# Recurrent layer: the score products of a chunk as two products of 64 stationary columns each

## The chip, the cores and the metric

The kernel runs on one core of a Trainium2 chip. The metric is the device time of one execution in microseconds; shown are the median of three runs and one execution under the hardware profiler, which gives the trace. TensorE is called PE in the profile (its weight loads PEld), VectorE DVE, ScalarE ACT, GpSimd POOL, SyncE SP.

## The reference, cut to what matters

A streaming encoder of two layers, 512 positions of width 1024. Layer 0 mixes by RWKV-7 (12 heads of 64) beside an attention into 256 memory tokens, layer 1 by chunked attention; each is followed by a conv-GLU. The change lies in the recurrent mixer of layer 0:

```python
def step(state, inp):
    r_t, w_t, k_t, v_t, a_t, b_t = inp
    sa = jnp.einsum('bhvk,bhk->bhv', state, a_t)
    state = (state * w_t[:, :, None, :] + sa[..., None] * b_t[:, :, None, :]
             + v_t[..., None] * k_t[:, :, None, :])
    return state, jnp.einsum('bhvk,bhk->bhv', state, r_t)
...
_, ys = lax.scan(step, s0, xs)
```

## The kernel before, in words

The kernel doesn't step through positions. It cuts the 512 positions into 8 chunks of 64 and makes, for each chunk and head, the four 64 by 64 score blocks between the keys (b and k, divided by the decay) and the queries (a and r, times the decay); the state then goes from chunk to chunk. Two heads make a pair, head 0 in partitions 0 to 63 and head 1 in partitions 64 to 127, and there are six pairs.

Each pair goes through three generators. `prepare` (line 574) projects r, k, v, and fills the tiles `AR` (queries: slot 0 is a, slot 1 is r) and `KB` (keys: slot 0 is k, slot 1 is b, slot 2 a copy of k, made by ScalarE on line 659); it also inverts the small triangular blocks on VectorE, lines 665 to 677, with transfers to DRAM and back around them. `front` (line 715) makes the score products on line 725, masks them with the constant `m1` into the tile `ML` on VectorE (line 728), and transposes keys, queries and values on lines 739, 749 and 751. `back` (line 776) makes the products with `ML` (among them lines 789, 797, 813, 824), runs over the chunks and hands the pair on.

On line 725 the stationary operand of one product is 64 partitions by 128 columns: two neighbouring slots of `KB`, slots 1 and 2 (b, k) for head 0 and slots 0 and 1 (k, b) for head 1. The moving operand is `AR` with both slots, 128 columns. The output is one of two PSUM banks, one for each head, 128 partitions by 128 columns for each of four chunks. So b lands in the head's own partitions and k in those of the other head. `front` runs the loop twice, for chunks 0 to 3 and 4 to 7 (`c4`); this makes 16 products a pair and 96 in all. All operands are fp32. Lines 749 and 751 are of another shape: 64 stationary and 64 moving columns, the first with the output in the head's own partitions, the second with it in the other head's.

`weave` (line 82) interleaves the generators by costs that are written beside each `yield`: in each of five stages it runs `back` of pair i-1, `front` of pair i and `prepare` of pair i+1. The framework then places the instructions on each engine by its own priorities and dependences; on each engine they run in the order so fixed. The pool `ps_s`, of which the score products take two banks, has four banks while this layer runs. The layer's remainder on TensorE is dense products (`dense`, lines 198, 199, 203), which take the projections of the next pair.

Of the kernel before, what the change touches and what calls it, by code (L numbers as in the profile page):

```python
# [111 lines left out]
def trunk_kernel(ctx, tc, A, out):  # L112
    nc = tc.nc
    PE, V, SC, GP = nc.tensor, nc.vector, nc.scalar, nc.gpsimd
# [19 lines left out]
    def C(name, lo=0, n=None):  # L134
        o, w = COFF[name]
        return cst[:, o + lo:o + lo + (w if n is None else n)]
# [7 lines left out]
    def ps_s(shape=(P, S)):  # L144
        return banks["S"].tile(list(shape), F32, name="pss", tag="pss")
# [7 lines left out]
    def ups():  # L153
        return ps_s((P, 8, 64))
# [224 lines left out]
    HS = (top, bot)  # L379
# [26 lines left out]
    def kt_(name, shape=(P, S), bufs=None, dt=F32):  # L406
        if bufs is None:
            return kp.tile(list(shape), dt, name=name, tag=name)
        return kp.tile(list(shape), dt, name=name, tag=name, bufs=bufs)
# [139 lines left out]
    def c3(ap):  # L549
        return ap.rearrange("p (c t) -> p c t", c=NCH)  # L550
# [164 lines left out]
    def front(i, T):  # L715
        v, KB, AR, Tt = c3(T["v"]), T["KB"], T["AR"], T["Tt"]

        ML = kt_("ML", (P, 2, NCH, 192), bufs=2)

        for c4 in range(2):  # L720
            ps = [ps_s((P, 4, 128)) for _ in range(2)]
            for c in range(4):
                cc = c4 * 4 + c
                for h in range(2):
                    PE.matmul(ps[h][:, c], KB[HS[h], cc, 1 - h:3 - h].rearrange("p s t -> p (s t)"),
                              AR[HS[h], cc].rearrange("p s t -> p (s t)"), start=True, stop=True)
            for h in range(2):
                V.tensor_tensor(ML[:, h, c4 * 4:c4 * 4 + 4, 0:128], ps[h][:],  # L728
                                C("m1").unsqueeze(1).to_broadcast([P, 4, 128]), op=ALU.mult)
            yield 1000  # L730
        Rq = kt_("Rq", (P, 8, 64), bufs=2)
        SC.copy(Rq[:], AR[:, :, 1, :])
        VT = kt_("VT", (P, 3, NCH, 64), bufs=2)

        def rows_kb():
            ps = [ups(), ups()]
            for c in range(8):
                for h in range(2):
                    PE.transpose(ps[h][:, c], KB[HS[h], c, 1 - h:3 - h].rearrange("p s t -> p (s t)"),
                                 cst[HS[h], I64:I64 + 64])  # L740
            for h in range(2):
                SC.copy(ML[:, h, :, 128:192], ps[h][:])


        def rows_av():
            ps = [ups(), ups()]
            for c in range(8):
                for h in range(2):
                    PE.matmul(ps[h][HS[h], c], AR[HS[h], c, 0], cst[HS[h], I64:I64 + 64], start=True, stop=True)
                for h in range(2):  # L750
                    PE.matmul(ps[h][HS[1 - h], c], v[HS[h], c], C("blkc", h * 64, 64)[HS[h]], start=True, stop=True)
            for h in range(2):
                SC.copy(VT[:, h], ps[h][:])

        rows_av()
        yield 1000
        rows_kb()
        yield 800
        T.update(Rq=Rq, ML=ML, VT=VT)
# [157 lines left out]
    for st_ in range(NPAIR - 1):  # L917
        gens = [(front(st_, Ts[st_]), 1.069 * FRONT_COST), (prepare(st_ + 1, Ts[st_ + 1]), .971 * PREP_COST)]
        if st_ > 0:
            gens.insert(0, (back(st_ - 1, Ts[st_ - 1], dst_mix), 1.003 * BACK_COST))  # L920
        weave(gens, tc)
# [39 lines left out]
    def later(ns):  # L961
        yield 0, ns

    a_, b_ = NPAIR - 2, NPAIR - 1
    weave([(told(back(a_, Ts[a_], dst_mix), "back"), 1.5 * BACK_COST),
           (chain(front(b_, Ts[b_]), later(25000), back(b_, Ts[b_], dst_mix, other_tiles, lambda: "back" in over)),
            1.5 * (FRONT_COST + BACK_COST)),
           (told(chain(q_mem(lambda f: A["wA"][18 + f], hact, qmA), flush_mix(), mA), "mem"),
# [336 lines left out]
```

## Time and profile before

| | us |
|---|---|
| median of three runs (lowest, highest) | 1363.49 (1362.89, 1365.41) |
| the profiled execution | 1366.57 |
| its span in the trace | 1364.8 |
| TensorE busy in the span | 1316.1 |
| VectorE busy in the span | 825.4 |
| ScalarE busy in the span | 615.1 |

A row of a timeline merges neighbouring instructions of one line: its length goes from the first start to the last end, and x16 says that it holds 16 records. An fp32 product leaves two records, each with a weight load of its own. Matmul starts are measured, their ends are modelled, so that the distance between starts tells more than the length of one record. "128*64 64x128" in a row is the stationary operand's partitions and columns, then the moving operand's. The stage of the recurrent layer lies between some 84 and 350 us.

### The profile page before, as it was taken

What the parts mean: (1) busy time and instruction counts of PE and PEld (TensorE: products, weight loads), DVE (VectorE), ACT (ScalarE), POOL (GpSimd) and SP (SyncE); (2) the same over time, 40 slices, a digit from 0 to 9 for tenths busy, and PEclk for the clock granted to TensorE, in tenths of its full rate; (3) what the DMA queues carried; (4) which work ended last, traced back from release to release, by engine and by line L of the source; (5) the groups of instructions that cost most, each with busy time, mean ns of one, the idle gap of its engine ahead of it and who ended that gap; (6) DMA issues with size and microseconds to landing.
All of it is one profiled execution on the core that took longest, in us unless ns stands there. A gap on an engine that the chain in (4) does not pass through costs nothing.

```text
span 1364.8 us, 20881 instructions
## 1 busy us (share of the span) xinstructions
PE 1316.1 (96%) x8266; PEld 1070.6 (78%) x8266; DVE 825.4 (60%) x1751; ACT 615.1 (45%) x1025; POOL 35.5 (3%) x57
## 2 busy tenths in 40 slices
PE   6989999999999999999999999999999999999996
PEld 5777777776788888888888878786888888888886
DVE  7876888778475556555334675757666555653324
ACT  6556565555444333333222476657443333332221
POOL 3000000000000000000000000000000000000000
PEclk9999999999999999999999999999999999999998
DMA  5366544555222322232233422232322232233332
GB/s 183 113 188 130 108 99 106 116 109 132 81 91 93 102 100 93 94 106 88 85 87 112 131 86 93 86 116 63 108 93 93 95 106 93 93 94 88 106 85 75
DMA packets 64322, 140.49 MB, mean 103 GB/s; under 512 B 24672, under 2 KB 28896, under 8 KB 64224
## 3 DMA queue, kind: packets, MB, share of 16 engines
q1 hardware_dynamic: 61200, 128.15, 30.0%
q0 software_dynamic: 3024, 11.01, 4.6%
q8 instruction: 65, 1.06, 0.3%
q14 instruction: 33, 0.27, 0.1%
HBM read 132.32 MB, written 6.82 MB: 102 GB/s over the span
## 4 chain that ended last, share of the span: by engine, by line
PE 78%; DVE 12%; ACT 4%; DMA 3%; issue 2%; SPq 1%; DVEq 0%; ACTq 0%; POOLq 0%
PE psf L198 12%; PE psf L199 12%; PE psf L203 12%; PE psd L198 10%; PE psd L199 10%; PE psd L203 10%; DVE Xu L675 2%; DVE Xs L677 1%; PE pss L1122 1%; PE psl L203 1%; DVE Xs L670 1%; DVE ML L728 1%; PE pss L297 1%; PE psd L1072 1%; PE pss L1108 1%
## 5 line engine op out<-in xcount | busy, mean ns | idle before, releaser
L175 DVE TENSOR_TENSOR wlo<-wraw,whi 128x1024 fp32r<-128x1024 f32 (+1 forms) x181 | 216.5, 1196 | 132.5 <-PE psd L203 118.2
L169 ACT CAST whi<-wraw 128x1024 fp32r<-128x1024 f32 (+1 forms) x202 | 207.8, 1030 | 162.2 <-DMA wraw<-in_ffn_out_dram 40.1
L198 PE MATMUL psf<-r2h,whi 128*128 128x512 f32 x352 | 137.1, 390 | 0.0
L198 PE MATMUL psf<-r1h,whi 128*128 128x512 f32 x352 | 137.1, 390 | 0.0
L199 PE MATMUL psf<-r1l,whi 128*128 128x512 f32 x352 | 137.0, 389 | 0.0
L199 PE MATMUL psf<-r2l,whi 128*128 128x512 f32 x352 | 136.9, 389 | 0.0
L198 PE MATMUL psd<-r1h,whi 128*128 128x512 f32 x318 | 127.4, 401 | 1.2 <-ACT whi L169 1.2
L199 PE MATMUL psd<-r1l,whi 128*128 128x512 f32 x318 | 124.9, 393 | 0.0
L203 PE MATMUL psd<-r1h,wlo 128*128 128x512 f32 x318 | 86.7, 405 | 4.4 <-DMA wlo<-in_wA_dram 4.4
L199 PE MATMUL psd<-f3l,whi 128*128 128x512 f32 (+1 forms) x238 | 88.6, 377 | 0.0
L198 PE MATMUL psd<-f3h,whi 128*128 128x512 f32 (+1 forms) x238 | 88.5, 376 | 0.0
L362 DVE TENSOR_TENSOR tmp<-psf,rho 128x512 f32<-128x512 f32 x44 | 30.4, 692 | 94.7 <-PE psf L203 94.7
L203 PE MATMUL psf<-r1h,wlo 128*128 128x512 f32 x352 | 86.9, 389 | 0.0
L203 PE MATMUL psf<-r2h,wlo 128*128 128x512 f32 x352 | 86.9, 389 | 0.0
L198 PE MATMUL psd<-r2h,whi 128*128 128x512 f32 (+1 forms) x200 | 77.1, 389 | 0.8 <-ACT r2h L1129 0.7
L199 PE MATMUL psd<-r2l,whi 128*128 128x512 f32 (+1 forms) x200 | 76.3, 384 | 0.8 <-DVE r2l L216 0.8
L203 PEld LDWEIGHTS psf<-r2h,wlo 128*128 128x128 f32 x352 | 66.1, 188 | 13.7
L199 PEld LDWEIGHTS psf<-r1l,whi 128*128 128x128 f32 x352 | 66.1, 188 | 13.7
L203 PEld LDWEIGHTS psf<-r1h,wlo 128*128 128x128 f32 x352 | 66.1, 188 | 13.7
L199 PEld LDWEIGHTS psf<-r2l,whi 128*128 128x128 f32 x352 | 66.1, 188 | 13.7
L198 PEld LDWEIGHTS psf<-r2h,whi 128*128 128x128 f32 x352 | 66.1, 188 | 13.6
L198 PEld LDWEIGHTS psf<-r1h,whi 128*128 128x128 f32 x352 | 66.1, 188 | 13.6
(369 smaller groups left out, 2442.3 us busy)
## 6 DMA issues: line engine op xcount, KB each, us to landing
wraw<-in_ffn_in_dram SPq DMA_DIRECT2D x88, 512.0 KB, 3.2
wraw<-in_ffn_out_dram SPq DMA_DIRECT2D x32, 448.0 KB, 3.3
wraw<-in_wA_dram SPq DMA_DIRECT2D x20, 512.0 KB, 3.9
wlo<-in_wA_dram POOLq DMA_DIRECT2D x17, 512.0 KB, 7.9
wraw<-in_w_out_dram SPq DMA_DIRECT2D x16, 512.0 KB, 3.4
wraw<-in_ffn_out_dram SPq DMA_DIRECT2D x16, 512.0 KB, 4.5
wraw<-in_wB_dram SPq DMA_DIRECT2D x8, 512.0 KB, 3.3
Lr<-d SPq DMA_DIRECT2D x24, 128.0 KB, 5.4
```

What stands on the lines that cost most here:

```text
L169: SC.copy(hi[:, :n], raw)
L175: V.tensor_tensor(lo[:, :n], raw, hi[:, :n], op=ALU.subtract)
L198: PE.matmul(ps, wh[:, j * P:(j + 1) * P], ah, start=start and n == 0, stop=False)
L199: PE.matmul(ps, wh[:, j * P:(j + 1) * P], al, start=False, stop=False)
L203: PE.matmul(ps, wl[:, j * P:(j + 1) * P], act(k)[0], start=False, stop=stop and n == len(ks) - 1)
L297: PE.matmul(pso[hs, :], vm[l][:, kt, (f * 2 + hh) * 64:(f * 2 + hh + 1) * 64], pts[f, hh, kt], start=kt == 0, stop=kt == 1)
L362: V.tensor_tensor(v[:], pv[:], rho[:], op=ALU.mult)
L670: V.scalar_tensor_tensor(X[:, m, q + 1:], L1[:, :, 0], X[:, m, q:q + 1], X[:, m, q + 1:], op0=ALU.mult, op1=ALU.add)
L675: V.tensor_tensor(uv, L1.rearrange("p i o -> p o i").to_broadcast([P, k, n]), X[:, 0:k, q:q + 1].to_broadcast([P, k, n]), op=ALU.mult)
L677: V.tensor_tensor(X[:, 0:k, q + 1:], X[:, 0:k, q + 1:], uv, op=ALU.add)
L728: V.tensor_tensor(ML[:, h, c4 * 4:c4 * 4 + 4, 0:128], ps[h][:], C("m1").unsqueeze(1).to_broadcast([P, 4, 128]), op=ALU.mult)
L1072: PE.matmul(pt, r1h[:, k, ts], wh[:, ws], start=k == 0, stop=False)
```

## The change

In `front`, each product of 128 stationary columns is made as two of 64. For `d` = 0, slot 1 (b) of both heads, with the output in the head's own partitions; for `d` = 1, slot 0 (k) of both heads, with the output in the other head's. The values, the banks and the place of each value stay; the number of products goes from 96 to 192. Slot 2 of `KB` is still read by line 739.

```diff
             for c in range(4):
                 cc = c4 * 4 + c
-                for h in range(2):
-                    PE.matmul(ps[h][:, c], KB[HS[h], cc, 1 - h:3 - h].rearrange("p s t -> p (s t)"),
-                              AR[HS[h], cc].rearrange("p s t -> p (s t)"), start=True, stop=True)
+                for d in range(2):
+                    for h in range(2):
+                        PE.matmul(ps[h][HS[h ^ d], c], KB[HS[h], cc, 1 - d],
+                                  AR[HS[h], cc].rearrange("p s t -> p (s t)"), start=True, stop=True)
             for h in range(2):
                 V.tensor_tensor(ML[:, h, c4 * 4:c4 * 4 + 4, 0:128], ps[h][:],
                                 C("m1").unsqueeze(1).to_broadcast([P, 4, 128]), op=ALU.mult)
```

## Rows read from the trace of the kernel before

**Rows 1.** The page, part 1: engine, busy us (share of the span), instructions.
```profile
PE 1316.1 (96%) x8266; PEld 1070.6 (78%) x8266; DVE 825.4 (60%) x1751; ACT 615.1 (45%) x1025; POOL 35.5 (3%) x57
```

**Rows 2.** Instructions of lines 725 and 813: ns min/median/max, first and last start.
```profile
L725 PEld LDWEIGHTS pss<-AR,xT x192: 182/188/334, 86.8 to 302.2; 64*128 64x128 f32 x192
L725 PE MATMUL pss<-AR,xT x192: 272/272/579, 86.8 to 302.3; 64*128 64x128 f32 x192
...
L813 PEld LDWEIGHTS pss<-VT,Tt x192: 129/133/133, 131.1 to 344.1; 64*64 64x64 f32 x192
```

**Rows 3.** Table by stretch: us, busy us of each engine, PEclk, DMA share, GB/s.
```profile
84.00:350.00 266.00, 249.04 (x3109) 192.68 (x3107) 206.70 (x714) 153.85 (x295) 17.41 (x20) 0.99 0.52 118
120.00:296.00 176.00, 168.13 (x2119) 129.89 (x2119) 139.52 (x489) 101.48 (x184) 11.22 (x13) 1.00 0.50 109
...
97.20:101.20 4.00, 4.00 (x21) 2.93 (x21) 0.00 (x0) 0.55 (x1) 0.16 (x1) 0.50 1.05 278
```

**Rows 4.** Chain that ended last, 84 to 350 us: its shares by line.
```profile
by line: DVE Xu L675 8.8%; DVE Xs L677 7.3%; PE psd L203 5.3%; DVE Xs L670 4.1%; issue 3.9%; DVE ML L728 3.8%; PE psd L198 3.5%; DMA wlo<-in_wA_dram 3.1%; PE psd L199 2.8%; DMA d<-Xs 2.6%; SPq L680 2.5%; DMA Lr<-d 2.5%; PE psl L844 2.1%; PE
```

**Rows 5.** Instructions of line 728, 84 to 350 us, and what they waited for.
```profile
L728 DVE TENSOR_TENSOR ML<-pss,cst x24: 679/684/695, 88.0 to 304.6; 128x512 f32<-128x512 f32 x24
...
  PE pss L725: 4.6, 2
...
DVE ML L728 <- PE pss L725: 4.6, 2, 4.2
```

**Rows 6.** Timeline of PE, 92 to 103 us: start, us, instruction, count, idle before.
```profile
97.18 2.07 PE L203 MATMUL psd<-r1h,wlo 128*128 128x512 f32 x4 [4.44 <-DMA wlo<-in_wA_dram]
99.18 2.08 PE L725 MATMUL pss<-AR,xT 64*128 64x128 f32 x16
101.19 1.90 PE L203 MATMUL psd<-r1h,wlo 128*128 128x512 f32 x4
```

**Rows 7.** Timeline of PE: one burst of lines 725, 813 and 824 each.
```profile
133.24 1.16 PE L725 MATMUL pss<-AR,xT 64*128 64x128 f32 x16
134.34 1.09 PE L813 MATMUL pss<-VT,Tt 64*64 64x128 f32 x16
...
139.21 1.96 PE L824 MATMUL pss<-ML,W 64*64 64x128 f32 x32
```

**Rows 8.** Timeline of PE: lines 749 and 751, first and last records; line 797.
```profile
108.16 0.27 PE L749 MATMUL pss<-cst,AR 64*64 64x64 f32 x2
108.17 0.27 PE L751 MATMUL pss<-cst,xT 64*64 64x64 f32 x2
108.27 0.22 PE L749 MATMUL pss<-cst,AR 64*64 64x64 f32 x2
108.28 0.23 PE L751 MATMUL pss<-cst,xT 64*64 64x64 f32 x2
108.33 0.23 PE L749 MATMUL pss<-cst,AR 64*64 64x64 f32 x2
108.34 0.23 PE L751 MATMUL pss<-cst,xT 64*64 64x64 f32 x2
...
109.10 0.22 PE L751 MATMUL pss<-cst,xT 64*64 64x64 f32 x2
...
126.67 1.15 PE L797 MATMUL pss<-VT,ML 64*64 64x64 f32 x32
```

**Rows 9.** Line 789: a burst in the timeline of PE, and its ns min/median/max.
```profile
211.89 0.69 PE L789 MATMUL pss<-Tl,ML 32*32 32x32 f32 x32
...
L789 PE MATMUL pss<-Tl,ML x160: 191/191/212, 121.9 to 298.2; 32*32 32x32 f32 x160
```

**Rows 10.** Timeline of PE, 122.4 to 124.9 us: order around one burst.
```profile
122.50 0.49 PE L725 MATMUL pss<-AR,xT 64*128 64x128 f32 x2
122.92 0.49 PE L696 MATMUL pss<-tmp,blk 128*128 128x512 f32 x1
123.34 1.16 PE L725 MATMUL pss<-AR,xT 64*128 64x128 f32 x14
```

## The prediction

> **What bounds the kernel now.** I read the page's share of busy time first: TensorE (PE) is busy 96% of the span, VectorE 60% [rows 1]. The bound is TensorE as a whole, but the change touches only line 725, and the shares of a stage are what count. The per-line view gives its place: 192 records between 86.8 and 302.3 us [rows 2]. In the stretch 84 to 350 us TensorE is busy 249.04 of 266 us, so 17 us are idle there, and 9.1 of these lie before 120 us or after 296 us: in 120 to 296 us it is 168.13 of 176 us [rows 3]. So inside the recurrent stage about 95 of each 100 ns taken off TensorE's queue have a chance to count.
>
> But a busy engine is not the same as a path. The chain of waits over that stretch is headed by VectorE's recurrence (lines 675, 677 and 670), and the product's reader, line 728, stands in it with 3.8% [rows 4]. Line 725 is named as what line 728 waited for only twice, 4.6 us in all [rows 5]. And 4.2 of these 4.6 us are one event, which I can place: TensorE idles 4.44 us for a weight transfer, the granted clock is then 0.50 (the lower level, 1.2 GHz) from 97.20 to 101.20 us, and the line-725 burst at 99.18 us takes 2.08 us in place of 1.16 [rows 3, 6, 7]. That wait belongs to a DMA and to the clock after an idle stretch, not to the shape of the products.
>
> **How a burst of line 725 runs today.** Each fp32 product shows as two records. A burst (four chunks, two heads) is 16 records and lasts 1.16 us from its first start to its last modelled end [rows 7]; there are 12 of them: eight in this form, three with the first product split off, one at the low clock. The last record alone is 0.27 us, so 15 distances between starts fill 0.89 us. The lines beside it give the pace: line 813 has the same 128 moving columns with 64 stationary ones, also 16 records, and takes 1.09 us; line 824, of the same form, takes 1.96 us for 32 [rows 7]. The 16 further records cost 0.87 us, 0.109 us for a pair, one record of each head. That the records of a pair run side by side and not after one another is seen in rows 8, where neighbours start 0.01 us apart and the next group 0.06 us later. So the array is full before the change: its upper 64 rows by 128 columns hold one head, the lower 64 rows the other. The change lets four products of half the width run in the place of two; it doesn't lower the number of columns that are streamed.
>
> **The change part by part.**
>
> *Removed: the wide weight loads.* A load of 128 stationary columns takes 188 ns (median) in line 725, one of 64 takes 133 ns in line 813 [rows 2]. Only the first load of a burst is exposed, since the following ones run beside products. Its gain is 188 - 133 = 55 ns a burst. The comparison of whole bursts says the same: 1.16 - 1.09 = 0.07 us [rows 7], 55 ns of it the first load and the rest, 15 ns over seven further pairs, the pairs' slightly closer spacing.
>
> *Added: 96 products, thus 192 records and 192 loads.* The trace of before has the exact form, at half the moving width: lines 749 and 751 put two heads on the diagonal quadrants and then on the other two, in the order in which the change does it. There the four records start at 108.16 and 108.17 us and the next four at 108.27 and 108.28, then at 108.33 and 108.34, 0.06 us a group; 64 records go from 108.16 to the last start at 109.10 us, plus 0.22 us [rows 8]. Line 797, with the same 64 moving columns on two quadrants only, takes 1.15 us for 32 records [rows 8]. So 64 records on four quadrants take 109.10 + 0.22 - 108.16 = 1.16 us, as long as 32 on two: the second pair is free except for about 0.01 us once at each burst's end. I take 0.02 us a burst for it, the upper end by these rows.
>
> *The sum on TensorE.* A burst goes from 1.16 to 1.09 + 0.02 = 1.11 us, 0.05 us less. Twelve bursts make 0.6 us, and the one at the low clock counts twice: 0.65 us.
>
> *What of this reaches the end.* Lower end 0: where VectorE's recurrence paces the step, the products only end 0.05 us earlier into a queue that is late anyway. Upper end 0.65 us: TensorE paces all. TensorE is busy 168.13 of 176 us, but VectorE leads the chain [rows 3, 4]; I lie nearer to the first and take 0.4 us.
>
> *What doesn't move.* Line 728 reads the same two banks with the same shape (684 ns, 24 of them) [rows 5]; the rows of a bank come in the same places, so ScalarE and VectorE get no new work, and no transfer is added. The third copy in the key tile is still needed by the transposes of line 739; only the products stop reading it. The loads and products of line 739, which follow, are unchanged.
>
> *A rule against it.* The row for the cost of a product that is too small to fill its slot is line 789's: 32 records of 32 columns in 0.69 us, of which 0.19 is the last record, so 0.50 us for 31 distances, 16 ns a record [rows 9]. That is a floor that a crowd of small products pays, and it is far under the 27 ns a record that four quadrants with 128 columns would need (0.109 us by four). The Trainium skill, TensorEngine Tiling (Array Packing), section Performance Considerations, says that every matmul carries an overhead of about 60 cycles and warns against tiling along a dimension that is already small. By that page, as an estimate, 192 more products of 60 cycles at 2.4 GHz would add 4.8 us; here the streamed dimension isn't made smaller, and the 64 records in 1.16 us speak against it.
>
> **Rivals.**
>
> *A, the order of TensorE's queue is drawn anew and comes out worse (slower).* The engines' orders are not those of the code: one product of a burst stands at 122.50 us, then a product of line 696, and the remaining 14 records from 123.34 us [rows 10]. The framework places each instruction by its own idea of when it is due, and 96 more products shift that idea for everything behind them. What such a placement can cost is shown by the event at 92 to 101 us: 4.44 us idle, and then 4.00 us at half clock, which loses 2.0 us [rows 3, 6]; 6.4 us together. One more such event gives 1363.5 + 6.4 = 1369.9; half of one, 1366.7. It decides from 2.7 us of additional idle time on TensorE between 84 and 350 us, where 17 us are now. For it: the slack is small and the stage couples five engines. Against: nine of the twelve bursts of line 725 keep together as they are written, and dense products stand around all of them that any order can use as filling.
>
> *B, the same redraw comes out better.* At most the event at 92 to 101 us goes away: 1363.5 - 6.4 = 1357.1; half, 1360.3. Nothing in the change shortens that transfer, so less likely than A.
>
> *C, the second pair does not run beside the first when 128 columns stream.* Both column halves read the same 64 rows' operand. If they take turns, each burst gets eight more pairs of 0.109 us, 0.87 us less the 0.05: 12 x 0.82 = 9.8 us, thus 1373.3. If they run side by side but each of the 192 added records shows the 16 ns of line 789 [rows 9], it is 3.1 us: 1366.6. (The overhead that the Trainium skill's tiling page states, above, would act in this way.) Rows 8 speak clearly against it; what is left is that the width there is 64.
>
> **How the numbers follow.** The profiled execution takes 1366.57 us, its span 1364.8, and the median of the three runs is 1363.49. The sum is 0.4 us off the profiled one, 1366.2, and likewise off the median: 1363.1. Chances: forecast 0.67 (1362.8 to 1363.5, and some 0.7 us to each side for the spread of a median), A 0.16, B 0.10, C 0.07. Low end 1360.0 and high end 1367.5 leave out the outer parts of A, B and C, about 2 in 10; the likeliest case alone holds 1362.1 to 1364.2. A run can tell about 0.2%, 2.7 us. Faster by more than that: B, 0.10. Slower: A and C, 0.23. The same: 0.67.
>
> **What the next profile would show.** Right: line 725 with 384 records of about 270 ns and loads of about 133, bursts of 32 records in 1.10 to 1.11 us, groups of four starts some 0.11 us apart. Wrong on C: bursts near 1.95 us. Wrong on A or B: the bursts are right, and TensorE's idle time between 84 and 350 us has moved by over 2.7 us from 17. If idle time and bursts stay and the time moves all the same, the bound was read wrongly.

## The result and the profile after

The changed kernel takes 1376.66 us (median of 22 runs, 1370.19 to 1383.08) against 1366.32 us for the kernel before on the same chip: ratio 1.0071, 95% interval 1.0057 to 1.0084. It is some 10 us slower; forecast was 0.4 us less, too little to tell from nothing. The profiled execution takes 1375.35 us, its span is 1373.6.

The page, part 1, and the product's own line (ns min/median/max, first and last start), with one burst from TensorE's timeline:

```profile
PE 1321.7 (96%) x8458; PEld 1074.5 (78%) x8458; DVE 825.6 (60%) x1751; ACT 616.1 (45%) x1025; POOL 35.2 (3%) x57
...
L726 PEld LDWEIGHTS pss<-AR,xT x384: 129/133/228, 86.3 to 305.3; 64*64 64x64 f32 x192
L726 PE MATMUL pss<-AR,xT x384: 268/269/473, 86.3 to 305.4; 64*64 64x128 f32 x192
...
168.12 1.10 PE L726 MATMUL pss<-AR,xT 64*64 64x128 f32 x32
```

The product (line 726 now; everything behind it moved down by one line) behaves as the change says: 384 records for 192, loads of 133 ns for 188 [rows 2], and a burst of 32 records in 1.10 us for 16 in 1.16 [rows 7]. The bursts show nothing of the loss. The stretches show where it is (us, busy us of each engine, PEclk, DMA share, GB/s), after:

```profile
84.00:350.00 266.00, 245.52 (x3129) 188.56 (x3129) 200.53 (x698) 149.08 (x280) 17.41 (x20) 0.95 0.52 118
...
166.00:208.00 42.00, 37.47 (x542) 29.82 (x542) 32.73 (x112) 23.90 (x44) 2.59 (x3) 0.96 0.43 93
208.00:252.00 44.00, 41.64 (x563) 33.02 (x562) 35.04 (x124) 25.09 (x45) 2.59 (x3) 0.96 0.46 100
252.00:296.00 44.00, 40.30 (x554) 31.95 (x554) 34.36 (x121) 24.52 (x44) 2.59 (x3) 0.96 0.48 102
...
324.00:328.20 4.20, 3.06 (x26) 2.07 (x27) 4.15 (x16) 2.04 (x8) 0.86 (x1) 1.00 0.69 166
328.20:341.90 13.70, 13.70 (x58) 7.53 (x56) 6.82 (x25) 6.71 (x22) 0.00 (x0) 0.50 0.36 70
```

Read the PEclk column, third from the end. Before, the clock was 0.99 between 84 and 350 us and 1.00 from 120 to 296 [rows 3]. Now it is 0.96 in each of three stages, and then 0.50 for 13.7 us on end, from 328.2 us. TensorE's idle time from 84 to 350 us is 266 - 245.52 = 20.5 us for 17.0. Three of its waits, from TensorE's timeline (the bracket is the idle time before the row, and who ended it):

```profile
183.49 1.05 PE L558 MATMUL pss<-cst,tmp 128*128 128x2 f32 x8 [1.75 <-ACT tmp L633]
...
272.15 1.05 PE L558 MATMUL pss<-cst,tmp 128*128 128x2 f32 x8 [1.84 <-ACT tmp L633]
...
326.15 0.33 PE L845 MATMUL psl<-W,MQ 64*64 64x64 f32 x4 [1.14 <-DVE W L846]
```

None of the three is at a score product. Line 558 sums squared keys of the pair that is being prepared; line 845 is the chunk-to-chunk recurrence of `back`. Soon behind each the clock is at half; for the third that is the last row of the table above, for the other two these:

```profile
184.90:188.20 3.30, 3.30 (x92) 3.18 (x84) 2.98 (x23) 1.07 (x2) 0.00 (x0) 0.50 0.12 26
273.70:277.00 3.30, 3.30 (x86) 3.18 (x80) 3.02 (x22) 1.07 (x2) 0.00 (x0) 0.50 0.09 19
```

The stage between these two has a fourth stretch, 3.4 us long. It comes behind a wait of 0.89 us at line 750:

```profile
229.24:232.66 3.42, 3.42 (x92) 3.30 (x94) 3.42 (x23) 1.07 (x2) 0.00 (x0) 0.50 0.02 7
```

The four together are some 24 us at half clock. Between 84 and 120 us there are some 3 us less of it than before (PEclk 0.95 for 0.91 over 36 us). Half of the 21 us that are left is 10 us. As an estimate, this is as much as the whole loss, if TensorE sets the pace throughout.

The mask behind the score products waits once for them, 3.5 us, for twice, 4.6 us, before [rows 5]; it is no part of the loss:

```profile
DVE ML L729 <- PE pss L726: 3.5, 1, 3.5
```

### The profile page after: what moved, and what is told of

Read it like the earlier page. It is cut to its first block, busy times and chain, and to the rows that moved or that the text cites. A ratio compares the mean times of both kernels' runs of the same rounds, so it can differ in the third digit from the quotient of the medians.

```text
span 1373.6 us, 21264 instructions
## 1 busy us (share of the span) xinstructions
PE 1321.7 (96%) x8458; PEld 1074.5 (78%) x8458; DVE 825.6 (60%) x1751; ACT 616.1 (45%) x1025; POOL 35.2 (3%) x57
## 4 chain that ended last, share of the span: by engine, by line
PE 77%; DVE 11%; DMA 4%; ACT 4%; issue 2%; SPq 1%; DVEq 0%; ACTq 0%; POOLq 0%
PE psf L198 12%; PE psf L199 12%; PE psf L203 12%; PE psd L198 10%; PE psd L199 9%; PE psd L203 9%; DVE Xu L675 1%; PE pss L1123 1%; DMA d<-Xs 1%; DVE Xs L677 1%; DVE Xs L670 1%; PE psl L203 1%; DVE ML L729 1%; SPq L680 1%; PE pss L297 1%
## 5 line engine op out<-in xcount | busy, mean ns | idle before, releaser
L203 PE MATMUL psd<-r1h,wlo 128*128 128x512 f32 x318 | 86.4, 404 | 4.4 <-DMA wlo<-in_wA_dram 4.4
L203 PE MATMUL psf<-r1h,wlo 128*128 128x512 f32 x352 | 86.9, 389 | 0.0
L203 PE MATMUL psf<-r2h,wlo 128*128 128x512 f32 x352 | 86.9, 389 | 0.0
L198 PEld LDWEIGHTS psf<-r1h,whi 128*128 128x128 f32 x352 | 66.1, 188 | 13.7
L203 PEld LDWEIGHTS psf<-r1h,wlo 128*128 128x128 f32 x352 | 66.1, 188 | 13.7
L203 PEld LDWEIGHTS psf<-r2h,wlo 128*128 128x128 f32 x352 | 66.1, 188 | 13.7
L198 PEld LDWEIGHTS psf<-r2h,whi 128*128 128x128 f32 x352 | 66.1, 188 | 13.7
L199 PEld LDWEIGHTS psf<-r2l,whi 128*128 128x128 f32 x352 | 66.1, 188 | 13.6
L199 PEld LDWEIGHTS psf<-r1l,whi 128*128 128x128 f32 x352 | 66.1, 188 | 13.6
```

Of the source, the lines that this page charges most:

```text
L198: PE.matmul(ps, wh[:, j * P:(j + 1) * P], ah, start=start and n == 0, stop=False)
L199: PE.matmul(ps, wh[:, j * P:(j + 1) * P], al, start=False, stop=False)
L203: PE.matmul(ps, wl[:, j * P:(j + 1) * P], act(k)[0], start=False, stop=stop and n == len(ks) - 1)
```

## The experiments

**The form or the order?** Theory: the form is innocent; the framework, given 96 more products, set other orders on the engines, and these cost the time. Rival: the form does something to its neighbours that the burst doesn't show. Two kernels have their instructions chained in a listed order, which fixes what an engine issues next and adds no wait:

```diff
         trunk_kernel(tc, aps, out)
+        pin_order(nc, tc)
...
+            if last is not None:
+                tc.add_manual_dep(made[e][k], last.name,
+                                  mybir.DependencyInfo(mybir.DependencyClass.NoSync, mybir.DependencyReason.DATA),
+                                  reason="order")
+            last = made[e][k]
```

The first is the changed kernel with every engine in the order of the kernel before:

> The changed products (64 stationary columns, four quadrants), with the instructions of every engine held in the order that the kernel before had; nothing else differs. Theory (the order): all of the loss comes from the order in which the framework queued the work once 96 products were added; the products themselves are 0.05 us a burst cheaper. Then this run is 0 to 0.65 us faster than the kernel before, ratio 0.9995 to 1.000, the bursts of line 726 take some 1.10 us, and the granted clock is at half only where it was in the kernel before (one stretch near 96 us). Rival (the form): 64-column products lower the clock or slow their neighbours whatever the order. Then ratio near 1.007 and half-clock stretches near 185, 229, 274 and 328 us as in the changed kernel.

The second is the kernel before, wide products and all, in the changed kernel's order:

> The products of the kernel before (128 stationary columns), with every engine held in the order that the changed kernel has. Theory (the order): slower than the kernel before by the loss of the changed kernel and the 0.05 us a burst that the wide products cost, 9.7 + 0.65 = 10.4 us, ratio 1.0076, with four additional stretches at half clock. Rival (the form): ratio 1.000, half clock only near 96 us.

Pairs are counted from 0; the texts on record also call them layers. Measured: 1.0002 (0.9992 to 1.0012, 12 runs) for the first and 1.0060 (1.0041 to 1.0078) for the second. Stretches of the first, with one of its waits, and then of the second, same columns as above:

```profile
84.00:350.00 266.00, 246.13 (x3279) 191.16 (x3280) 205.84 (x712) 153.78 (x294) 17.41 (x20) 0.98 0.51 118
...
208.00:252.00 44.00, 42.78 (x565) 34.11 (x565) 35.92 (x130) 24.84 (x45) 2.59 (x3) 0.96 0.51 111
...
296.00:324.00 28.00, 23.89 (x423) 18.80 (x421) 23.54 (x82) 13.01 (x25) 1.72 (x2) 1.00 0.56 157
...
328.20:341.90 13.70, 13.70 (x133) 8.61 (x131) 8.79 (x35) 8.98 (x27) 0.00 (x0) 1.00 0.25 50
...
298.50 0.66 PE L567 MATMUL pss<-cst,tmp 128*128 128x128 f32 x4 [2.01 <-DVE tmp L564]
```

```profile
324.00:328.20 4.20, 4.20 (x33) 2.80 (x28) 4.14 (x17) 2.50 (x10) 0.00 (x0) 0.68 0.89 153
328.20:341.90 13.70, 13.70 (x51) 6.72 (x50) 4.41 (x15) 6.21 (x18) 0.00 (x0) 0.60 0.20 43
...
323.73 0.33 PE L844 MATMUL psl<-W,MQ 64*64 64x64 f32 x4 [1.06 <-DVE W L845]
```

With new products and the old order, the clock stays at 1.00 through the recurrence; with old products and the new order the wait is back (323.73 us, 1.06 us) and the low clock with it. That settles the first question: the order carries the loss, with either form.

Two things in the first kernel are easily read past. Its stage from 208 us shows 0.96 as well, so the fourth stretch of after comes with the old order too, and what brings it was not tried. And TensorE idles 266 - 246.13 = 19.9 us in it, nearly as long as after, with one wait of 2.01 us, and loses no time that can be measured. So idle time alone isn't the loss.

**Which places?** All four kernels have the new products; three repair the new order, one spoils the old. The first repair: in the new order the last r-projection record (L203, 176.58 us) stands behind the second burst, and its reader on VectorE (L605, 179.09) behind both masks; in the old order L605 ran at 177.05, ahead of the masks. In pairs 3 and 5 both go ahead again:

```diff
+PE   L203  psd<-r1h,wlo   (last record)
 PE   L726  second burst
-PE   L203  psd<-r1h,wlo   (last record)
...
+DVE  L605  tmp<-psd,rho
 DVE  L729  ML<-pss,cst
 DVE  L729  ML<-pss,cst
-DVE  L605  tmp<-psd,rho
```

> The changed kernel in its own order, except at two places (near 176 and 265 us): the last dense product of a projection (line 203) stands ahead of the second burst of score products, not behind it, and its reader on VectorE (line 605) ahead of the two maskings (line 729). Theory (order, idle time, clock): TensorE's two waits of 1.75 and 1.84 us at line 558 shrink to under 1 us and the half-clock stretches at 185 and 274 us, 3.41 us each, go; 1.7 us each for the clock and about 1 us each for the wait, 5 us in all, of which perhaps 1 to 2 us are given back to a later wait: ratio to the kernel before 1.003 to 1.0045. Rival (the form lowers the clock): the stretches at half clock stay, ratio near 1.006 to 1.007.

Measured: 1.0080 (1.0058 to 1.0102), no gain. Its waits, from the timeline:

```profile
171.34 1.11 PE L567 MATMUL pss<-cst,tmp 128*128 128x128 f32 x4 [2.92 <-DVE tmp L564]
...
189.07 1.05 PE L558 MATMUL pss<-cst,tmp 128*128 128x2 f32 x8 [1.25 <-ACT tmp L633]
...
170.40:177.30 6.90, 5.96 (x73) 4.39 (x73) 3.67 (x9) 2.27 (x5) 0.00 (x0) 0.51 0.00 0
```

L558 still waits, 1.25 us in place of 1.75, a larger wait stands ahead of it, and half clock comes with both (6.9 us from 170.4 us, 3.4 us from 190.9 us). So this pair of moves isn't, or isn't alone, what makes L558 late. Which instruction's place does was not found.

The second repair moves one VectorE step (the first L846 of pair 4) seven places ahead:

> The changed kernel in its own order, except that one instruction on VectorE near 325 us (the first state step of line 846 in the last but one pair) stands seven places earlier, ahead of two residual splits and a maximum. Theory (order, idle time, clock): TensorE's wait of 1.14 us at 326.15 us goes and with it the stretch at half clock from 328 to 342 us, 13.65 us long, which costs up to 6.8 us; ratio to the kernel before 1.002 to 1.003. Rival 1 (the wait alone counts, the clock falls anyway): 1 us, ratio 1.0063. Rival 2 (form): nothing moves, 1.007.

Measured: 1.0069 (1.0052 to 1.0086). TensorE's timeline, and the stretch behind:

```profile
328.52 0.33 PE L845 MATMUL psl<-W,MQ 64*64 64x64 f32 x4
...
331.39 0.44 PE L845 MATMUL psl<-W,MQ 64*64 64x64 f32 x4 [1.36 <-DVE W L846]
...
331.40:345.20 13.80, 13.80 (x63) 8.15 (x64) 7.69 (x28) 6.28 (x23) 0.00 (x0) 0.51 0.39 73
```

The step that was moved is in time (no bracket at 328.52), and the next one waits 1.36 us, with the same 13.8 us at half clock behind it. The wait had only moved on by one.

The third takes the new order up to pair 5's inversion (line 652) and the old order from there:

> The changed products; up to the first L652 product of layer 5 (283.0 us in the changed kernel) every engine in the changed kernel's order, from there in the order of the kernel before. If the loss is made stage by stage, each by its own order: the head keeps what it costs (half clock at 184.9, 229.2 and 273.6 us, 3 x 1.7 us, and some 2 us of waits, against nothing but one such stretch before) and the tail's 13.65 us at half clock are gone (6.8 us): ratio 1.001 to 1.004. If what the tail loses is handed down from the head (VectorE late from there on), the tail's order helps nothing: 1.006 to 1.008.

Measured: 1.0026 (1.0008 to 1.0044), as the stage-by-stage theory had it.

```profile
166.00:208.00 42.00, 37.47 (x531) 29.97 (x530) 32.06 (x115) 22.41 (x41) 1.73 (x2) 0.92 0.44 100
...
252.00:296.00 44.00, 41.01 (x561) 32.43 (x560) 35.09 (x123) 24.73 (x45) 2.66 (x4) 0.96 0.47 103
...
328.20:341.90 13.70, 13.70 (x94) 8.31 (x95) 8.90 (x33) 9.40 (x32) 0.00 (x0) 1.00 0.49 99
341.90:370.00 28.10, 28.10 (x341) 21.10 (x340) 12.55 (x37) 14.23 (x32) 0.86 (x1) 0.88 0.12 41
```

The head still shows 0.92 and 0.96; the 13.7 us are at full clock, though some 7 us behind them are not (0.88 in 28.1 us). (This execution took 1373.84 us; the median of the ten is 1368.95.) By the ratios about 0.0045 of the 0.0071 lie in the tail, give or take 0.002, and the head isn't what slows the tail.

Last the opposite, and the smallest edit of all: the old order, in which one instruction of VectorE goes two places later.

```diff
 DVE  L677  Xs<-Xs,Xu
-DVE  L846  W<-psl,dE,VT   (pair 4, first step)
 DVE  L270  mst<-pss
 DVE  L270  mst<-pss
+DVE  L846  W<-psl,dE,VT   (pair 4, first step)
```

> The changed products with every engine in the order of the kernel before, but for one instruction: on VectorE the first state update of layer 4 (L846, 322.8 us) goes two places later, behind two maxima of the memory attention (L270, 1.28 us together). Theory 1: TensorE's wait at its next state product grows from 0.40 us to some 1.7 us, the clock falls soon after as it does at 328 us in the changed kernel, and the time rises by 1.3 us and half of the stretch (3.41 to 13.65 us): ratio 1.002 to 1.006. Theory 2: only the wait is added: 1.001.

Measured: 1.0083 (1.0058 to 1.0108). VectorE, TensorE and the stretches:

```profile
324.88 1.28 DVE L270 TENSOR_REDUCE mst<-pss 128x2 f32<-128x512 f32 x2
326.08 0.28 DVE L846 SCALAR_TENSOR_TENSOR W<-psl,dE,VT 128x64 f32<-128x64 f32 x1
...
326.41 0.42 PE L845 MATMUL psl<-W,MQ 64*64 64x64 f32 x4 [1.59 <-DVE W L846]
...
326.50:343.60 17.10, 17.10 (x76) 9.81 (x76) 7.44 (x27) 6.64 (x23) 0.00 (x0) 0.50 0.32 63
```

1.28 us of other work ahead of one step, a wait of 1.59 us (0.37 in the first experiment's kernel, which differs by this move alone), and then 17.1 us at half clock: 1.2 us of waiting and, as an estimate, half of 17.1, 8.6 us, of slowness. The edit costs as much as the whole change. More came than theory 1 allowed (1.006 at most), in part since I had not reckoned with a stretch longer than the one of after.

**The wait or the clock?** A kernel whose VectorE is just as late, but whose TensorE has something to do meanwhile, parts the two. Products of a constant are put on TensorE's queue ahead of the waiting ones; they go to columns that are written anew or never read.

```diff
         ps = bank()
+        for _ in range(fill):
+            filling(PE.matmul(ps[:, P:2 * P], C("ident"), C("ident"), start=True, stop=True))
...
+            if i == 4 and c == 2:
+                for _ in range(4):
+                    filling(PE.matmul(psc[:, 7], C("ident"), C("ident", 0, 64), start=True, stop=True))
```

> The changed kernel, each engine in the changed kernel's own order, with repeated 128x128 products of a constant put on TensorE's queue ahead of three waits of its trace: three ahead of the head-sum products of L558 in layers 3 and 5 (waits of 1.75 and 1.84 us, half clock 3.41 us each time right after) and four of 64 columns ahead of the third state product of layer 4 (L845, wait of 1.14 us, half clock for 13.65 us from 2 us later). Nothing else moves, the waits stay, and the products go to columns that are written anew or never read. Theory 1 (the time goes to the lower clock, and the clock falls because TensorE stood idle): the stretches from 184.9, 273.6 and 328.2 us are gone, 3.41/2 + 3.41/2 + 13.65/2 = 10.2 us less: ratio to the kernel before 0.999 to 1.002. Theory 2 (the time goes to the waits themselves and the clock falls for reasons of its own): the ratio stays at 1.006 to 1.008.

Measured: 1.0076 (1.0052 to 1.0099): as theory 2 had it, but not all the waits were filled. Its timeline, and the places of the three stretches:

```profile
181.98 0.94 PE L565 MATMUL pss<-cst 128*128 128x128 f32 x6
183.81 1.05 PE L567 MATMUL pss<-cst,tmp 128*128 128x2 f32 x8 [0.89 <-ACT tmp L642]
...
270.39 1.05 PE L567 MATMUL pss<-cst,tmp 128*128 128x2 f32 x8 [1.00 <-ACT tmp L642]
...
323.39 1.10 PE L855 MATMUL psl<-cst 128*128 128x64 f32 x8 [1.14 <-DVE W L859]
...
184.90:188.20 3.30, 3.30 (x92) 3.18 (x94) 3.23 (x23) 1.07 (x2) 0.00 (x0) 0.50 0.11 24
273.70:277.00 3.30, 3.14 (x41) 2.49 (x38) 3.13 (x17) 1.48 (x3) 0.00 (x0) 1.00 0.00 0
324.80:338.40 13.60, 13.60 (x64) 8.50 (x60) 7.70 (x28) 5.38 (x20) 0.00 (x0) 0.50 0.41 76
```

Three products filled half of the wait at line 558 (567 in this kernel), and the fill in the recurrence (L855) itself waited 1.14 us for the step that it was to bridge; it writes the tile that this step reads. With 0.89 and 1.00 us of the waits left at line 567, the clock fell behind the first and not behind the second. In the recurrence the filling products ran behind the wait, and 13.6 us at half clock followed as before: it isn't their mere presence that keeps the clock up. So it was made again: six products for three, and in the recurrence products with a stationary of zeros, added to the other accumulator:

```diff
-                    filling(PE.matmul(psc[:, 7], C("ident"), C("ident", 0, 64), start=True, stop=True))
+                    filling(PE.matmul(psy[:, 0], zero[:], C("ident", 0, 64), start=False, stop=False))
```

> As e5 (the changed kernel in its own order), with the fills large enough and able to run: six products instead of three ahead of L558 in layers 3 and 5 (three took 0.94 us of the 1.75), and at the third state product of layer 4 four products of a stationary of zeros added to the other accumulator (psy), which no VectorE step reads, so that they can run inside the wait of 1.14 us; in e5 they waited for the same VectorE step as the product itself. Theory 1 (standing idle lowers the clock): no half clock from 184.9, 273.6 and 324 to 328 us, up to 10.2 us less: ratio 0.999 to 1.002. Theory 2 (the clock falls there for other reasons): stretches at the same places, ratio 1.006 to 1.008.

Measured: 1.0024 (1.0014 to 1.0034), for 1.0071 of the same order unfilled.

```profile
321.82 0.83 PE L857 MATMUL psl<-cst,zero 128*128 128x64 f32 x6
...
166.00:208.00 42.00, 40.08 (x566) 31.46 (x565) 34.12 (x119) 24.94 (x45) 2.59 (x3) 1.00 0.49 105
...
252.00:296.00 44.00, 41.82 (x572) 33.01 (x572) 34.85 (x125) 24.98 (x45) 2.60 (x3) 1.00 0.50 107
...
324.00:342.00 18.00, 17.79 (x190) 11.19 (x189) 12.17 (x46) 11.41 (x37) 0.00 (x0) 1.00 0.32 61
```

All three stretches are at full clock, in the order that had the late steps. The difference, 0.0047 or 6.4 us, is what filling the waits gave back. What is left, 0.0024 or some 3 us, is the lateness and the filling products themselves; no run parts the two. Theory 1's upper end, 1.002, lies inside the interval.

The same on the kernel with one late step, six products of zeros in its wait:

> As e8 (order of the kernel before, one state update of layer 4 two places later on VectorE; its wait of 1.59 us was followed by 17.07 us at half clock, ratio 1.0083), with six products of 64 columns of zeros, some 1.6 us, on TensorE's queue ahead of the product that waits. The chain of VectorE is as late as in e8. Theory 1: no half clock at 326 us, 8.5 us less: ratio 1.001 to 1.003. Theory 2 (the late VectorE step costs the time, or the clock falls whatever TensorE does in the wait): 1.007 to 1.009.

Measured: 1.0018 (1.0006 to 1.0031), for 1.0083 unfilled.

```profile
321.29 1.55 PE L854 MATMUL psl<-cst,zero 128*128 128x64 f32 x12
...
324.40:338.70 14.30, 14.30 (x123) 8.90 (x122) 8.98 (x32) 7.57 (x23) 0.00 (x0) 1.00 0.28 55
338.70:345.60 6.90, 6.90 (x82) 5.49 (x82) 2.81 (x14) 3.40 (x11) 0.00 (x0) 0.51 0.01 2
```

On VectorE the step still stands behind both maxima, in the same order, and 1.55 us of useless products save some 9 us.

**A version that beats both?** The kernel before has one such place as well, the transfer at 97 us, behind which it runs at 0.50 [rows 3, 6]. In the old order with the new products, nine and then 18 products of zeros (`psd<-cst,zero`) were put ahead of that L203 group:

> The changed products with every engine in the order of the kernel before (ratio 1.0002 without more), and nine products with a stationary of zeros, added to the running sum, ahead of the L203 group at 97 us, where TensorE waits 4.4 to 4.8 us for the DMA of wlo, and where half clock stands from 96 us for 6.83 us. Theory 1: the stretch at 96 us is gone and 6.83/2 = 3.4 us with it: ratio 0.997 to 0.998, so that this kernel is faster than both. Theory 2: the ratio stays at 1.000.

> As e6 (changed products, order of the kernel before), with 18 instead of nine products of zeros ahead of the L203 group of layer 1 (nine took 2.17 us, and 2.03 us of the wait were left). Theory 1: TensorE no longer stands idle there and the stretch at 96 to 98 us is gone: ratio 0.997 to 0.999 (3.4 us less at most, against e1's 1.0002). Theory 2: the stretch stays, ratio 1.000 to 1.002.

Measured: 1.0019 (1.0002 to 1.0035) and 1.0008 (0.9997 to 1.0019); theory 1 had expected 0.997 to 0.998 and 0.997 to 0.999, and missed. TensorE's timeline and stretches of the second:

```profile
92.67 4.18 PE L212 MATMUL psd<-cst,zero 128*128 128x128 f32 x36
97.24 1.23 PE L214 MATMUL psd<-r1h,wlo 128*128 128x512 f32 x4 [0.39 <-DMA wlo<-in_wA_dram]
...
97.20:105.00 7.80, 7.70 (x59) 5.78 (x59) 4.48 (x16) 3.38 (x5) 0.86 (x1) 1.00 0.96 244
...
319.00:335.80 16.80, 16.42 (x146) 10.25 (x146) 11.96 (x43) 10.75 (x36) 0.00 (x0) 1.00 0.44 94
335.80:342.60 6.80, 6.80 (x78) 5.39 (x76) 2.90 (x13) 3.36 (x11) 0.00 (x0) 0.50 0.00 0
```

The wait is filled, and the place at 97 us runs at 1.00. But in this execution the clock falls at 335.8 us, where it hadn't in the kernel before, after 16.8 us with only 0.4 us idle; the kernel with one late step, filled, does the same at 338.7. Over all runs the mean granted clock is 0.9917, as good as the 0.9914 without the fill. In this execution, what was gained at one place was lost at another; why is open. No kernel here beats the one before.

**All runs together.** For each run the result lists span and mean granted clock; the means:

| kernel | span, us | clock | product, us |
|---|---|---|---|
| before, beside the two order kernels (17 runs) | 1364.4 | 0.9919 | 1353.3 |
| after (22) | 1374.9 | 0.9843 | 1353.3 |
| new products, old order (12) | 1364.7 | 0.9914 | 1353.0 |
| old products, new order (6) | 1372.5 | 0.9870 | 1354.6 |
| one step late (4) | 1374.4 | 0.9852 | 1354.2 |
| one step late, filled (10) | 1366.5 | 0.9908 | 1353.9 |
| new order, filled (9) | 1366.7 | 0.9918 | 1355.5 |

The product is the span as it would be at full clock throughout, if TensorE set the pace all the time. It stays within 2.5 us while the spans differ by 10.5; the kernels not listed lie between 1353.3 and 1354.7. So most of what these orders cost is the clock, and the waits themselves cost one or two microseconds. The clock also differs between executions of one kernel (0.979 to 0.992 over the 22 of after), and each table of stretches shows a single one.

## Why the prediction was wrong, point by point

- **The step that failed.** The sum had no term for a redrawn order, and the likeliest case (0.67) took it as worth nothing. The new order with the old products measured 1.0060, some 8 us, most of it lost to the granted clock behind waits of a microsecond or two.
- **The burst.** Right: a whole burst takes 1.10 us for a forecast 1.10 to 1.11, loads of 133 ns, records of 269. The 0.4 us that were to reach the end are within the first experiment's interval (0.9992 to 1.0012 is -1.1 to +1.6 us), which can't tell them from nothing.
- **Rival C** (quadrants take turns, or each record shows a cost of its own) fell: 64-column products with 128 moving columns pack as those with 64 do. The overhead for each product that the Trainium skill, TensorEngine Tiling (Array Packing), section Performance Considerations, states does not show here: 4.8 us was the estimate from that page's figure, none shows in the bursts. (The estimate counted the 192 added records; the added products are 96.)
- **Rival A is what happened**, as the first two experiments show. Its own test, idle time, doesn't: after idles 20.5 us for 17.0, over the 2.7 us that it named, but the first experiment's kernel idles 19.9 us and loses nothing. The sign to name would have been the granted clock, 0.95 from 84 to 350 us for 0.98 there. Three steps of the rival failed. *The chance*, 0.16, leaned on the bursts' keeping together and on dense products around them. They did stay together but for the first records of five and for the last burst, which is torn by a wait of 0.99 us (304.55 us) that the first experiment's kernel has too; the loss arose at lines 558 and 845, where the late operand came from ScalarE and VectorE. I had looked at how well the changed line was covered, and not at how thin the cover is of other waits that an order touches. *The price* was one event like that at 92 to 101 us, most of it idle time (4.44 of 6.4 us). (Its half clock was read too short: PEclk is 0.88 from 92 to 97.2 us and 0.72 from 101.2 to 104 us in before, so that some 6.8 us are at half clock, not 4.00.) The events that came were the other way round: waits of 1.1 to 1.8 us with 3.4 to 13.7 us at half clock behind, 17.1 in the kernel with one late step. *The number*: one event at most, in a code of six pairs that repeats the same steps; two waits at line 558 came in the same form in two pairs, and one in the recurrence.
- **The range** (to 1367.5) cut through rival A, whose own end was 1369.9; the median of after lies above even that.
- **What bounds the kernel.** "TensorE as a whole" was right, and it has a consequence that I did not draw: where TensorE is busy 96%, its clock is part of the bound (the 17.1 us at half clock and the wait before them cost some 9 us). The row with 0.50 was in front of me [rows 3], and I used it only as the price of one transfer's wait.

## What to carry to other kernels

Adding instructions to a kernel whose framework sets the orders can redraw those of several engines: before a small gain is believed or a loss is put down to the edit, run the new form in the old order and the old form in the new one. Where TensorE is the bound, put the granted clock beside every wait in the table of stretches, since a wait of a microsecond can bring ten at half clock; and where such a wait can't be taken away, idle products in it can be worth more than they cost (1.55 us of them gave back some 9 us in the recurrence; at 97 us they brought nothing).

## What the runs showed that I had not expected

- Waits that look alike end differently. 1.59 us at line 845 are followed by 17.1 us at 0.50; in the kernel with new products and old order TensorE is idle for 4.1 of the 28 us from 296 to 324 us, 2.01 us of them at once, and the clock stays at 1.00. What else has to differ between the places was not tried by itself.
- The clock also falls with hardly any wait (335.8 us, 338.7 us, above). So in the recurrence one late step brings it about, and filling the wait keeps it away, but a wait isn't the only cause.
- The Trainium skill, TensorE: Matmul & The Clock Gate, section A second HAM failure mode: psum-queue depth-cycling, tells of a kernel whose many short idle times make the clock swing between its two levels. These traces agree in part: in after, three waits of 1.1 to 1.8 us stand ahead of stretches at 0.50, but they are single waits, and behind the one of 2.01 us above the clock stays at 1.00.
- Products with a stationary of zeros did as well as those of a constant: with 1.55 us of them in the wait the clock stayed at 1.00 for the 14 us behind it.
